# One w2 GEMM of a hybrid encoder layer: sums made in earlier jobs, and low parts moved between VectorE and adding transfers

## The chip, the cores and the metric

The kernel runs on one core of a Trainium2 chip. The metric is the device time of one execution in microseconds (us), as the median of several runs. The engines are named as the profile names them: PE (TensorE matmul), PEld (TensorE weight load), DVE (VectorE), ACT (ScalarE), POOL (GpSimd) and SP (SyncE, which here only issues transfers).

## What is computed

One layer of an encoder with 512 tokens of width 1024. It has two SwiGLU blocks, a recurrent branch and an attention branch. The change lies in the second SwiGLU block (FFN 2), which ends the layer:

```python
def swiglu(x, w1, w3, w2):
    return (jax.nn.silu(x @ w1) * (x @ w3)) @ w2

f = swiglu(rms_norm(h, ffn2_pre_g[l]), ffn2_w1[l], ffn2_w3[l], ffn2_w2[l])
h = h + 0.5 * rms_norm(f, ffn2_post_g[l])
```

Everything is float32; w1 and w3 are 1024 x 2816, w2 is 2816 x 1024. The hidden width is 22 blocks of 128, called f = 0 to 21.

## The kernel before

**Precision.** PE multiplies rounded operands. To keep float32 accuracy each operand is split into a high part (a rounded copy, made by ScalarE) and a low part (what the rounding left, made by VectorE as source minus high part: `split2`, L213 and L214). A product is three matmuls: high by high, low by high, high by low. A low part can also be made without VectorE: ScalarE writes the negated high part (or negated source), and a transfer issued by GpSimd adds the source onto it (`accum_op=ALU.add`, L610 and L613).

**Pair jobs.** w1 and w3 of FFN 2 run as 20 jobs of `Pairs` (f = 2 to 20 in steps of two, w1b and w3b in turn). Each job is a 2 x 2 block product in seven half-size products instead of eight, with sums of the weight blocks made by GpSimd (`S12`, `S34`) and split by ACT and DVE. `prep(m, i)` prepares a piece of the operands of job m and is called in the job before. Hooks (`late[n, i]`) run in job n behind its first, second or third product. The last job's hooks and its two `tail()` calls each ran `ahead`, which prepares one unit of the next stage; four units have slots of their own (`U_SLOTS`).

**w2 in halves.** `Halves` does the same seven-product scheme for w2 of FFN 2, with five groups of four hidden blocks (G = 5, `GS_B`), so 35 units, in the order m1, m5, m2, m6, m3, m7, m4 (`NAMES_B`). Units are numbered through: m1 is 0 to 4, m5 5 to 9, m2 10 to 14, m6 15 to 19, m3 20 to 24, m7 25 to 29, m4 30 to 34. The hidden blocks 20 and 21 (`TAIL_B`) are done by ordinary matmuls (`classical`). For each unit `prep` loads weight blocks (`raw_w2b`, 512 KB each), makes the high part `whi` (L607), the low part `wlo` (L615, or by transfer at L610 to L613) and the two parts of the x operand (`hx` for the first four units, then places in `uT`), and then `sums` makes, in place, the weight differences (T, L548: 128x1024) and the x sums (S, L551: 128x512) that later units need. For m1 that is T1 (b12 minus b11) and the sum s1. A unit is 12 matmuls of 512 columns (L640 to L642). `step(u)` prepares unit u + 5 (`LEAD`), runs the hooks of u and then the matmuls of u.

**What sets the order.** Nothing is reordered by a scheduler: each engine runs its instructions in the order in which the code issues them. Tiles in SBUF come from 42 equal slots (`NSLOT`), given out first in, first out: a new tile waits for the last use of the tile that had its slot before.

**The end.** `last_gemm` runs units 0 to 24, then for token tiles 0 and 1 the classical part, one or two preparations (units 29 and 30, then unit 31) and the norm of that tile (`post_norm`, L294 to L308, with ScalarE's squares at L296 and root at L259, and two output stores at L722). Then come m7 (units 25 to 29, in which units 32 and 33 are prepared and the last two tiles of h are loaded, L690), half of the classical part of token tiles 2 and 3, and `out("m7")` on VectorE (L652), which reads the PSUM banks that m4 then adds to. m4 runs twice, once for each of the token tiles 2 and 3 (six matmuls a unit); unit 34 is prepared when the first of the two begins. Each run of m4 is followed by the rest of that tile's classical part and its norm.

In this kernel m6's units 17 to 19 get their low parts by adding transfers (`M6_DMA`), m2's all five too, and m4's are made by VectorE.

Of the kernel before, what the change touches and what calls it, by code (L numbers as in the profile page):

```python
# [13 lines left out]
ALU = mybir.AluOpType  # L14
# [37 lines left out]
def hybrid_layer(ctx: ExitStack, tc: tile.TileContext, a: dict, out: bass.AP):  # L52
# [10 lines left out]
    def slot(shape, dt=F32, name="s"):  # L63
        uid[0] += 1
        return sb.tile(shape, dt, tag="slot", name=f"{name}_{uid[0]}")
# [9 lines left out]
    def f32(ap):  # L75
        return ap.bitcast(F32)
# [61 lines left out]
    raws, pairs = {}, {}  # L138
# [10 lines left out]
    def dma_to(n):  # L149
        while st["dma"] < min(n, len(order)):  # L150
            dma_one(st["dma"])
            st["dma"] += 1
# [11 lines left out]
    def split_to(n):  # L164
        while st["split"] < min(n, len(order)) and st["split"] not in paired:
            k = st["split"]
            dma_to(k + 1)
            r = raws.pop(k)
            if order[k] in BY_DMA:
                nm, i = order[k]  # L170
                pairs[k] = split_dma(r, a[nm][i * P : (i + 1) * P, :])
            else:
                hi = slot([P, D], F32R, name="whi")
                lo = slot([P, D], F32R, name="wlo")
                if order[k] in BY_POOL:
                    pool.tensor_copy(hi, r)
                else:
                    act.activation(hi, r, AF.Copy)
                dve.tensor_tensor(out=lo, in0=r, in1=f32(hi), op=ALU.subtract)
                pairs[k] = (hi, lo)  # L180
            st["split"] += 1
# [29 lines left out]
    def split2(hi, lo, src):  # L211

        act.activation(hi, src, AF.Copy)  # L213
        dve.tensor_tensor(out=lo, in0=src, in1=f32(hi), op=ALU.subtract)  # L214
# [276 lines left out]
    class Hidden:  # L491

        def __init__(self, seq):
            self.seq, self.f, self.t, self.done, self.eo = seq, {}, {}, 0, {}
# [21 lines left out]
    class Halves:  # L516
# [5 lines left out]
        def __init__(self, nm, hid, hooks, gs, names):  # L522
            self.nm, self.hid, self.hooks, self.gs, self.names = nm, hid, hooks, gs, names
            self.G = G = len(gs)
            self.loads = [(b, i) for bs in (("b11", "b12"), ("b22", "b21")) for i in range(G) for b in bs]
            if G > 4:
                self.loads[2 * G :] = [(b, i) for b in ("b22", "b21") for i in range(G)]
            self.cast_at = names.index("m3") * G - 5
            self.raw, self.ops, self.loaded, self.ready = {}, {}, 0, 0
            self.bank, self.c, self.accs, self.cast = {}, {}, {}, {}  # L530

        def src(self, b, i):
            src = a[self.nm]
# [19 lines left out]
        def t2(self, i):  # L553
            self.T("b22", "b22", "b12", i)
            del self.raw["b12", i]

        def sums(self, m, i):

            if m == "m1":
                self.T("b12", "b12", "b11", i)  # L560
                self.S((0, 1), (0, 1), (1, 1), i, ALU.add)
            elif m == "m5":
                if i < T2_EARLY:
                    self.t2(i)
                self.S((0, 0), (0, 1), (0, 0), i)
            elif m == "m2":
                if i >= T2_EARLY:
                    self.t2(i)
                self.T("b11", "b22", "b11", i)
                self.S((1, 0), (1, 0), (0, 0), i)  # L570
            elif m == "m6":
                self.S((0, 1), (1, 1), (0, 0), i)
                if self.G > 4:
                    self.T("b21", "b21", "b22", i)
                    del self.raw["b22", i]
            elif m == "m7":
                if self.G == 4:
                    self.T("b21", "b21", "b22", i)
                    del self.raw["b22", i]
                del self.raw["b11", i]  # L580
            elif m == "m4":
                del self.raw["b21", i]

        def prep(self, n):

            G = self.G
            while self.ready < min(n, 7 * G):
                u = self.ready
                self.ready += 1
                m, i = self.names[u // G], u % G  # L590
                self.load(min(4 * G, 2 * G + 1 + u))
                b, odd, half = self.OPERANDS[m]
                again = m == "m3" and G > 4
                hi = self.cast.pop(i) if m == "m3" and not again else slot([P, 2, 512], F32R, name="whi")
                lo = slot([P, 2, 512], F32R, name="wlo")
                if u < U_SLOTS:
                    xs = slot([P, 2, 2, 256], F32R, name="hx")
                else:
                    xs = uT[:, :, (u + 1) % 8, :].rearrange("p e (j c) -> p e j c", j=2)
                if again:  # L600
                    split2(hi, lo, self.cast.pop(i))
                elif m == "m3":
                    act.activation(lo, f32(hi), AF.Copy, scale=-1.0)
                    pool.dma_start(out=lo, in_=self.src(b, i), accum_op=ALU.add)
                else:
                    src = self.raw[b, i]
                    act.activation(hi, src, AF.Copy)  # L607
                    if m == "m2":
                        act.activation(lo, src, AF.Copy, scale=-1.0)
                        pool.dma_start(out=lo, in_=self.src(b, i), accum_op=ALU.add)  # L610
                    elif m == "m6" and i >= self.G - M6_DMA * (G > 4):
                        act.activation(lo, f32(hi), AF.Copy, scale=-1.0)
                        pool.dma_start(out=lo, in_=src, accum_op=ALU.add)  # L613
                    else:
                        dve.tensor_tensor(out=lo, in0=src, in1=f32(hi), op=ALU.subtract)  # L615
                split2(xs[:, 0, :, :], xs[:, 1, :, :], self.x(i, odd, half))
                self.ops[u] = hi, lo, xs
                if self.cast_at <= u < self.cast_at + G:
                    n = u - self.cast_at
                    if G > 4:  # L620
                        self.cast[n] = slot([P, 2, 512], name=f"raw_{self.nm}")
                        sp.dma_start(out=self.cast[n], in_=self.src("b22", n))
                    else:
                        self.cast[n] = slot([P, 2, 512], F32R, name="whi")
                        pool.dma_start(out=self.cast[n], in_=self.src("b22", n))
                self.sums(m, i)
# [53 lines left out]
    def blocks(nm, hid, pairs, late, h_src, gs, names, marks):  # L680

        hooks = {u: [] for u in range(7 * len(gs))}

        def tail_tile(n):
            hid.to(n + 1)
            split_to(st["get"] + n + 1)

        def h_back(t):
            h[t] = slot([P, D], name="h")
            sp.dma_start(out=h[t], in_=h_src(t))  # L690

        for at_, fn in zip(marks, (lambda n: dma_to(st["get"] + n + 1), tail_tile, h_back)):
            for n, u in enumerate(at_):
                hooks[u].append(lambda n=n, fn=fn: fn(n))
        half = Halves(nm, hid, hooks, gs, names)
        pairs.more = lambda n: half.load(LOAD_PAIRS[n])
        ahead = lambda: half.prep(half.ready + 1)
        end = len(pairs.jobs) - 1
        late[end, 1], late[end, 2 if pairs.R is None else 3] = [ahead], [ahead]
        pairs.run(ahead, late)  # L700
        return half

# [561 lines left out]
    def keep(u):  # L1264
        f, i = u // 2, u % 2
        if f not in kept:
            kept[f] = slot([P, 2, SEQ], name="kept")
        act.activation(kept[f][:, i, :], ps[u], AF.Copy)
# [34 lines left out]
    late = {(0, 1): [lambda: keep(2 * NC1 - 1)], (1, 1): [bias_in], (2, 3): [bias_parts], (3, 1): [bias_rows]}  # L1303
# [5 lines left out]

    h.clear()  # L1310
    half = blocks("w2a", hid, pairs_a, late, lambda t: a["x"][t * P : (t + 1) * P, :], GS_A, NAMES_A, MARKS_A)
    X1 = pairs_a = late = None
    for fn, at_ in zip((gate_kept, silu_kept, swiglu_kept), KEPT_AT):
# [5 lines left out]
    half = None  # L1319
# [185 lines left out]
    for t in range(NT):  # L1505
# [3 lines left out]
        for k in range(KT):  # L1509
            wh, wl = wv[k // 4]  # L1510
            s = slice((k % 4) * 256, (k % 4 + 1) * 256)
# [223 lines left out]
    late = {(0, 1): [lambda: X2.update(t4=to_uT(tn[3], 0, 1)), tn.clear]}  # L1735
    pairs_b.prep(1, 1)

    half = blocks("w2b", hid, pairs_b, late, lambda t: h_scr[t], GS_B, NAMES_B, MARKS_B)
    X2 = pairs_b = None
    last_gemm("w2b", hid, half, "ffn2_post_g", 0.5)  # L1740
# [29 lines left out]
LEAD = 5  # L1770
U_SLOTS = 4
LOAD_PAIRS = (0, 4, 6, 8)
GS_A = (1, 2, 3, 4)
NAMES_A = ("m1", "m5", "m2", "m6", "m7", "m3", "m4")
MARKS_A = (14, 16, 18, 20, 22, 24), (16, 18, 20, 22, 24, 26), (24, 25, 26, 27)
# [4 lines left out]
MARKS_B = (17, 18), (20, 22), (21, 22, 27, 29)  # L1780
GPOST_AT = 22
T2_EARLY = 3
M6_DMA = 3


RO = 6
# [59 lines left out]
```

## Time and profile before

| | |
|---|---|
| Median of 3 runs | 1113.86 us (1113.52 to 1114.41) |
| Profiled execution, its own time | 1112.68 us |
| Its span, first to last instruction | 1110.9 us |
| Granted TensorE clock, mean | 0.998 |
| First matmul of w2 of FFN 2 | 992.64 us from the span's start |
| Last matmul ends at | about 1104.2 us |

In the profile, a row of a timeline is: start, duration (both us), engine, line, operation, output and inputs, shape, and in brackets how long the engine had been idle before it and what ended that. A row of waits is: engine and line, what it waited for, total us, number of times, longest. A row of windows is: the window, its length, busy us (and instructions) of PE, PEld, DVE, ACT, POOL, then the granted clock, the share of the 16 DMA engines in use, and GB/s. A row of a transfer queue is: packets, MB, share of the 16 engines over the window. Recorded durations of DVE and ACT include an end that overlaps with the next instruction, so costs are taken from start to start.

### The profile page before, as it was taken

What the parts mean: (1) busy time and instruction counts of PE and PEld (TensorE: products, weight loads), DVE (VectorE), ACT (ScalarE), POOL (GpSimd) and SP (SyncE); (2) the same over time, 40 slices, a digit from 0 to 9 for tenths busy, and PEclk for the clock granted to TensorE, in tenths of its full rate; (3) what the DMA queues carried; (4) which work ended last, traced back from release to release, by engine and by line L of the source; (5) the groups of instructions that cost most, each with busy time, mean ns of one, the idle gap of its engine ahead of it and who ended that gap; (6) DMA issues with size and microseconds to landing.
All of it is one profiled execution on the core that took longest, in us unless ns stands there. A gap on an engine that the chain in (4) does not pass through costs nothing. (4 is left out here: it accounts for less than half of the span.)

```text
span 1110.9 us, 17989 instructions
## 1 busy us (share of the span) xinstructions
PE 1098.0 (99%) x6838; PEld 987.4 (89%) x6838; DVE 926.3 (83%) x1325; ACT 679.3 (61%) x1186; POOL 401.2 (36%) x332
## 2 busy tenths in 40 slices
PE   9999999999999999999999999999999999999996
PEld 7899999987788877899888888888999999997885
DVE  5888999999977978887778867767899898689995
ACT  7755556576747678666655664356455555567752
POOL 0143435602112423232556563010976665502000
PEclk9999999999999999999999999999999999999999
DMA  9325663477944542146122335442332323377712
GB/s 332 124 83 143 136 137 114 137 209 150 255 178 166 150 122 95 39 163 249 64 95 77 121 127 218 145 168 95 115 99 92 115 80 112 129 256 167 207 57 94
DMA packets 53061, 155.91 MB, mean 140 GB/s; under 512 B 5472, under 2 KB 7392, under 8 KB 52976
## 3 DMA queue, kind: packets, MB, share of 16 engines
q1 hardware_dynamic: 44128, 132.19, 34.5%
q0 software_dynamic: 8560, 22.07, 10.3%
q8 instruction: 53, 0.87, 0.3%
q10 hardware_dynamic: 288, 0.52, 0.1%
q14 instruction: 32, 0.26, 0.1%
HBM read 137.47 MB, written 13.62 MB: 136 GB/s over the span
## 5 line engine op out<-in xcount | busy, mean ns | idle before, releaser
L752 PE MATMUL c<-uT,wlo 128*128 128x256 f32 x516 | 146.0, 283 | 0.0
L753 PE MATMUL c<-uT,whi 128*128 128x256 f32 x516 | 146.0, 283 | 0.0
L751 PE MATMUL c<-uT,whi 128*128 128x256 f32 x516 | 146.0, 283 | 0.0
L752 PE MATMUL c<-Xh,wlo 128*128 128x256 f32 x504 | 142.8, 283 | 0.2 <-DVE wlo L214 0.2
L751 PE MATMUL c<-Xh,whi 128*128 128x256 f32 x504 | 142.7, 283 | 0.0
L224 PE MATMUL f<-uT,whi 128*128 128x512 f32 (+1 forms) x368 | 136.4, 371 | 0.0
L225 PE MATMUL f<-uT,wlo 128*128 128x512 f32 (+1 forms) x368 | 134.8, 366 | 0.0
L226 PE MATMUL f<-uT,whi 128*128 128x512 f32 (+1 forms) x368 | 134.8, 366 | 0.0
L753 PE MATMUL c<-Xl,whi 128*128 128x256 f32 x456 | 129.0, 283 | 0.0
L214 DVE TENSOR_TENSOR wlo<-S,whi 128x1024 fp32r<-128x1024 f32 x86 | 117.2, 1363 | 6.6 <-ACT whi L213 3.2
L213 ACT ACTIVATE whi<-S 128x1024 fp32r<-128x1024 f32 x86 | 88.5, 1054 | 33.2 <-DVE S L800 32.1
L752 PEld LDWEIGHTS c<-uT,wlo 128*128 128x128 f32 x516 | 99.0, 192 | 0.2
L751 PEld LDWEIGHTS c<-uT,whi 128*128 128x128 f32 x516 | 99.0, 192 | 0.2
L753 PEld LDWEIGHTS c<-uT,whi 128*128 128x128 f32 x516 | 99.0, 192 | 0.0
L752 PEld LDWEIGHTS c<-Xh,wlo 128*128 128x128 f32 x504 | 96.7, 192 | 0.5 <-DVE wlo L214 0.5
L751 PEld LDWEIGHTS c<-Xh,whi 128*128 128x128 f32 x504 | 96.7, 192 | 0.3 <-issue 0.3
L640 PE MATMUL hw<-whi,uT 128*128 128x512 f32 x220 | 85.9, 390 | 2.9 <-DVE hc L652 2.9
L753 PEld LDWEIGHTS c<-Xl,whi 128*128 128x128 f32 x456 | 87.5, 192 | 0.0
L641 PE MATMUL hw<-wlo,uT 128*128 128x512 f32 x220 | 86.5, 393 | 0.5 <-DMA wlo<-in_w2a_dram 0.2
L642 PE MATMUL hw<-whi,uT 128*128 128x512 f32 x220 | 86.3, 392 | 0.5
L224 PEld LDWEIGHTS f<-uT,whi 128*128 128x128 f32 x368 | 69.4, 189 | 12.5 <-issue 1.7
L226 PEld LDWEIGHTS f<-uT,whi 128*128 128x128 f32 x368 | 69.4, 189 | 11.4
(440 smaller groups left out, 3168.3 us busy)
## 6 DMA issues: line engine op xcount, KB each, us to landing
raw_w2b<-in_w2b_dram SPq DMA_DIRECT2D x27, 512.0 KB, 5.2
raw_w2a<-in_w2a_dram SPq DMA_DIRECT2D x22, 512.0 KB, 4.2
raw_w1b<-in_w1b_dram SPq DMA_DIRECT2D x22, 512.0 KB, 4.1
raw_w3b<-in_w3b_dram SPq DMA_DIRECT2D x22, 512.0 KB, 4.4
raw_w3a<-in_w3a_dram SPq DMA_DIRECT2D x21, 512.0 KB, 4.3
raw_w1a<-in_w1a_dram SPq DMA_DIRECT2D x20, 512.0 KB, 4.3
raw_wg<-in_wg_dram SPq DMA_DIRECT2D x16, 512.0 KB, 4.2
h<-in_x_dram SPq DMA_DIRECT2D x8, 512.0 KB, 7.3
```

Source lines behind the costliest of these rows:

```text
L213: act.activation(hi, src, AF.Copy)
L214: dve.tensor_tensor(out=lo, in0=src, in1=f32(hi), op=ALU.subtract)
L224: pe.matmul(ps[:, c0:c1], wh[:, s], h_, start=k == 0 and c0 == 0, stop=False, skip_group_check=True)
L225: pe.matmul(ps[:, c0:c1], wl[:, s], h_, start=False, stop=False, skip_group_check=True)
L226: pe.matmul(ps[:, c0:c1], wh[:, s], l_, start=False, stop=k == KT - 1, skip_group_check=True)
L640: pe.matmul(ps, xs[:, 0, j, c], hi[:, j, :], start=start and j == 0, stop=False, skip_group_check=True)
L641: pe.matmul(ps, xs[:, 0, j, c], lo[:, j, :], start=False, stop=False, skip_group_check=True)
L642: pe.matmul(ps, xs[:, 1, j, c], hi[:, j, :], start=False, stop=i == self.G - 1, skip_group_check=True)
L751: pe.matmul(ps, wh[:, s], xh, start=first, stop=False, skip_group_check=True)
L752: pe.matmul(ps, wl[:, s], xh, start=False, stop=False, skip_group_check=True)
L753: pe.matmul(ps, wh[:, s], xl, start=False, stop=k == 3, skip_group_check=True)
```

## The change

For w2 of FFN 2 alone (five groups; the four-group w2 of FFN 1 keeps its ways):

- The sums s1 of groups 0 to 3 and T1 of group 0 are made in the third pair job from the end, T1 of group 1 in the second from the end, T1 of group 2 in the last. `did` remembers them, so that `sums` leaves them out later; T1 of groups 3 and 4 and s1 of group 4 stay where they were.
- Unit 0 is prepared in the second job from the end, behind its second product, instead of in the last one. Units 1 to 3 follow in the last job.
- Six w2 loads are issued in the fourth job from the end (before: four at the end of the third from the end). The ones after that come later than before, relative to the units.
- m4's five low parts are made by a negation on ScalarE and an adding transfer, no longer by VectorE. m6's five are all made by VectorE; the three adding transfers there go.

```diff
+        def t1(self, i):
+            if ("t", i) not in self.did:
+                self.did.add(("t", i))
+                self.T("b12", "b12", "b11", i)
+
+        def s1(self, i):
+            if ("s", i) not in self.did:
+                self.did.add(("s", i))
+                self.S((0, 1), (0, 1), (1, 1), i, ALU.add)
+
         def sums(self, m, i):
             if m == "m1":
-                self.T("b12", "b12", "b11", i)
-                self.S((0, 1), (0, 1), (1, 1), i, ALU.add)
+                self.t1(i)
+                self.s1(i)
...
-        def prep(self, n):
+        def prep(self, n, load=True):
...
-                self.load(min(4 * G, 2 * G + 1 + u))
+                if load:
+                    self.load(min(4 * G, 2 * G + (u if u >= U_SLOTS else u == 3) if G > 4 else 2 * G + 1 + u))
...
-                    elif m == "m6" and i >= self.G - M6_DMA * (G > 4):
+                    elif m == "m4" and G > 4:
                         act.activation(lo, f32(hi), AF.Copy, scale=-1.0)
                         pool.dma_start(out=lo, in_=src, accum_op=ALU.add)
...
-        pairs.more = lambda n: half.load(LOAD_PAIRS[n])
-        ahead = lambda: half.prep(half.ready + 1)
+        pairs.more = lambda n: half.load((LOAD_PAIRS if len(gs) == 4 else LOAD_B)[n])
+        ahead = lambda: half.prep(min(half.ready + 1, U_SLOTS))
         end = len(pairs.jobs) - 1
         late[end, 1], late[end, 2 if pairs.R is None else 3] = [ahead], [ahead]
+        if pairs.R is None:
+            late[end - 3, 1] = [lambda: half.load(6)]
+            late[end - 2, 1] = [lambda i=i: half.s1(i) for i in range(len(gs) - 1)] + [lambda: half.t1(0)]
+            late[end - 1, 1] = [lambda: half.t1(1)]
+            late[end - 1, 2] = [lambda: half.prep(1, False)]
+            late[end, 1] = [lambda: half.t1(2)]
...
 LOAD_PAIRS = (0, 4, 6, 8)
+LOAD_B = (0, 6, 8, 10)
```

More of the change, by code (lines that the diff above doesn't have):

```diff
@@ L529, in __init__ @@
             self.raw, self.ops, self.loaded, self.ready = {}, {}, 0, 0
-            self.bank, self.c, self.accs, self.cast = {}, {}, {}, {}
+            self.bank, self.c, self.accs, self.cast, self.did = {}, {}, {}, {}, set()
         def src(self, b, i):
@@ L1782 @@
 T2_EARLY = 3
-M6_DMA = 3
 RO = 6
```

## The prediction

> **What bounds the kernel now.** The page first, then the waits of PE and of its weight loads in the last stage, then the timelines of that stage engine by engine, then its transfers.
>
> ```profile
> span 1110.9 us, 17989 instructions
> PE 1098.0 (99%) x6838; PEld 987.4 (89%) x6838; DVE 926.3 (83%) x1325; ACT 679.3 (61%) x1186; POOL 401.2 (36%) x332
> ...
> PE hw L640 <- DVE hc L652: 2.9, 1, 2.9
> ...
> PEld hw L641 <- DVE wlo L615: 1.3, 3, 0.5
> PEld hw L642 <- DVE uT L214: 1.2, 3, 0.4
> ...
> 1049.00:1069.00 20.00, 20.00 (x90) 16.57 (x89) 20.00 (x24) 14.37 (x20) 0.56 (x1) 1.00 0.23 80
> ```
>
> PE is the bound everywhere except in w2 of FFN 2 (from 992.6 us on). There VectorE (third busy time of the window's row) works 20.00 of 20 us, and PE waits for it: one stall of 2.9 us and six small weight-load waits, 2.5 us. More than some 5 us cannot be won.
>
> **The pair jobs, where work is added.**
>
> ```profile
> 962.42 1.68 POOL L804 TENSOR_TENSOR S<-raw_w3b 128x512 f32<-128x512 f32 x1 [1.49 <-DVE cc L874]
> ...
> 967.67 1.53 DVE L214 TENSOR_TENSOR wlo<-raw_w1b,whi 128x1024 fp32r<-128x1024 f32 x1 [4.73 <-ACT whi L213]
> ...
> 975.56 0.42 DVE L902 TENSOR_TENSOR hEO<-c,cc 128x256 f32<-128x256 f32 x1 [1.56 <-PE c L753]
> ...
> 977.28 2.00 ACT L213 ACTIVATE whi<-S 128x1024 fp32r<-128x1024 f32 x2
> ...
> 978.37 1.23 DVE L214 TENSOR_TENSOR wlo<-S,whi 128x1024 fp32r<-128x1024 f32 x1 [1.15 <-ACT whi L213]
> ...
> 981.74 0.42 DVE L874 TENSOR_TENSOR cc<-ct 128x256 f32<-128x256 f32 x1 [0.30 <-ACT ct L873]
> ...
> 984.12 1.23 DVE L615 TENSOR_TENSOR wlo<-raw_w2b,whi 128x1024 fp32r<-128x1024 f32 x1 [1.17 <-ACT whi L607]
> 985.27 0.68 DVE L214 TENSOR_TENSOR hx<-hEO,hx 128x512 fp32r<-128x512 f32 x1
> 985.87 1.22 DVE L548 TENSOR_TENSOR raw_w2b<-raw_w2b,raw_w2b 128x1024 f32<-128x1024 f32 x1
> 987.00 0.68 DVE L551 TENSOR_TENSOR hEO<-hEO,hEO 128x512 f32<-128x512 f32 x1
> ```
>
> Start to start, a 128x1024 operation takes 1.14 us and a 128x512 one 0.60. The third job from the end gets four x sums and one T1: 4 x 0.60 + 1.14 = 3.5 us, in a hole of 4.73. The one after gets a T1 in a hole of 1.56, then unit 0's two low parts (1.74); they push L902 back by about 1.7 us, and the 1.15 hole and the 0.30 one behind it take that up. So these cost PE nothing. Without the holes the cost would be their 6.4 us of queue.
>
> SP takes six w2 loads ahead of the last job's raw w3 weights. At under 0.5 us an issue (the row of the h loads below: 0.91 for two) that is under 3 us, for tiles that ScalarE reads over ten us later; nothing. The six loads hold six slots a job or two earlier: by my count of live tiles about 12 of the 42 are free there now, and about 5 would be. GpSimd's sums for the last job, which run a whole job ahead, then have to wait for slots (rival C).
>
> **How early VectorE gets.** In the last job it is held by what ScalarE has to do first.
>
> ```profile
> 987.34 0.39 ACT L850 ACTIVATE ct<-c 128x256 f32<-128x256 f32 x1
> ...
> 990.24 1.05 ACT L607 ACTIVATE whi<-raw_w2b 128x1024 fp32r<-128x1024 f32 x1
> ...
> 998.70 0.41 DVE L862 TENSOR_TENSOR cc<-c,ct 128x256 f32<-128x256 f32 x1
> ...
> 1000.42 1.22 DVE L615 TENSOR_TENSOR wlo<-raw_w2b,whi 128x1024 fp32r<-128x1024 f32 x1
> ...
> 1003.90 1.22 DVE L615 TENSOR_TENSOR wlo<-raw_w2b,whi 128x1024 fp32r<-128x1024 f32 x1
> ```
>
> Unit 2's high part still follows L850, which follows PE; unit 3's still starts at 990.24. So unit 3's low part starts at 991.35 at the earliest. Behind it: 1.14 + 0.60, T1 of unit 3 1.14, L862 to L902 1.72 (998.70 to 1000.42): unit 4 at 995.95, not 1000.42. Unit 4 keeps its T1 and sum (3.48, as from 1000.42 to 1003.90), so unit 5 starts at 999.4, not 1003.90. **Lead 4.5 us**, of 3 T1, 4 sums and one unit's splits, 7.6 us: the rest is lost in holes of the last job.
>
> Of the lead m6 takes three low parts that were transfers: 3 x 1.14 = 3.4. m4 gives one back before the first norm (unit 30): 1.1. At norm(0) VectorE is 4.5 - 3.4 + 1.1 = **2.2 us** earlier. The small PE waits mostly go, but PE isn't what is late:
>
> ```profile
> 1065.30 0.39 PE L244 MATMUL hw<-whi,hT 128*128 128x512 f32 x1
> ...
> 1069.78 0.68 DVE L294 TENSOR_TENSOR hc<-hw,hc 128x512 f32<-128x512 f32 x1
> ...
> 1078.07 0.68 DVE L294 TENSOR_TENSOR hc<-hw,hc 128x512 f32<-128x512 f32 x1
> ...
> 1086.79 1.28 DVE L652 TENSOR_TENSOR hc<-hw,hc 128x512 f32<-128x512 f32 x2
> ...
> 1087.62 0.47 PE L640 MATMUL hw<-whi,uT 128*128 128x512 f32 x1 [2.89 <-DVE hc L652]
> ```
>
> PE had the first token tile done at 1065.5, VectorE took it at 1069.78; from there to the stall the chain is VectorE's and ScalarE's.
>
> **From norm(0) to m4.** In m4 VectorE loses a 1.14 us low part per unit, and ScalarE gains a negation per unit.
>
> ```profile
> 1031.47 1.07 ACT L607 ACTIVATE whi<-raw_w2b 128x1024 fp32r<-128x1024 f32 x1 [0.40 <-DVE raw_w2b L548]
> 1032.57 1.06 ACT L612 ACTIVATE wlo<-whi 128x1024 fp32r<-128x1024 f32 x1
> 1033.54 0.61 ACT L213 ACTIVATE uT<-hEO 128x512 fp32r<-128x512 f32 x1
> ...
> 1074.32 1.04 ACT L607 ACTIVATE whi<-raw_w2b 128x1024 fp32r<-128x1024 f32 x1
> ...
> 1081.29 1.04 ACT L607 ACTIVATE whi<-raw_w2b 128x1024 fp32r<-128x1024 f32 x1
> ...
> 1083.71 0.61 ACT L213 ACTIVATE uT<-hEO 128x512 fp32r<-128x512 f32 x1
> ```
>
> m6 shows the form: negation 1.10 after the high part, x copy 0.97 after that, next unit 0.52 later, 2.59 us a unit instead of 1.47. Unit 31: high part at 1074.32 - 2.25 = 1072.07, x copy at 1074.14 to 1074.8, VectorE's x low part 0.60, norm(1) at 1075.4 instead of 1078.07: 2.67 earlier. Units 32 and 33 follow norm(1) on ScalarE: 1081.29 - 2.67 = 1078.62; unit 33's x copy at 1078.62 + 2.59 + 2.07 = 1083.28, done 1083.9. L652 is queued on VectorE behind that unit's x low part (1083.95 + 0.60): 1084.55 instead of 1086.79. m4 then starts at 1087.62 - 2.24 = **1085.38**. PE went idle at 1087.62 - 2.89 = 1084.73 and would, without some 1.9 us of small waits, at 1082.8: a stall of 2.5 us stays, and ScalarE is now its cause.
>
> **The adding transfers, the disputed term.** Unit 34's negation ends at 1078.62 + 2 x 2.59 + 1.10 + 1.06 = 1085.96; units 32 and 33 are 5.18 and 2.59 earlier.
>
> ```profile
> 1030.85 0.91 POOL L613 DMA_DIRECT2D wlo<-raw_w2b  x1 [4.71 <-ACT wlo L612]
> ...
> DMA to landing us min/median/max: 6.1/6.9/9.2
> ...
> 1010.99 1.26 POOL L610 DMA_DIRECT2D wlo<-in_w2b_dram  x1 [42.87 <-ACT uT L213]
> ...
> DMA  0000000000000000000058994966759366659599
> ...
> q0 software_dynamic: 432, 1.57, 57.4%
> ...
> 1083.85 0.91 SPq L690 DMA_DIRECT2D h<-h_scr  x2
> ...
> 1083.60:1088.20 4.60, 1.71 (x8) 1.11 (x8) 4.60 (x7) 2.19 (x4) 0.00 (x0) 1.00 0.98 337
> ...
> 1093.41 0.39 PE L641 MATMUL hw<-wlo,uT 128*128 128x512 f32 x1
> ```
>
> GpSimd issues 0.30 us after a negation (1032.57 is the second; the first ended at 1030.55, issue 1030.85). The digits are 0.1 us slices from 1010.9 us: the first bytes move 1.9 us after the issue. The q0 row covers 1032.7 to 1046.6: three transfers are 57.4% of 13.9 us, 2.66 us of all 16 engines each. Landing is 6.1 to 9.2 us after issue in m6, among reloads. In m4 the neighbours are norm(1)'s two output stores and the two loads of h, in the window's row 98% of all engines for 4.6 us; SP's order is kept, so with norm(1) they move to 1080.9 to 1085.5. Unit 32 issues at 1081.1, its bytes start at 1083.0, and 2.5 us of that traffic are still to come. Full engines then serve 2.5 + 3 x 2.66 = 10.5 us of work: 1093.5, and 0.3 to the landing (an estimate from the last m6 transfer): 1093.8. Unit 34's first L641 was 5.79 us behind m4's start (1093.41 - 1087.62) and so is due at 1091.17. It waits 2.7 us, to 1093.9 with 0.1 to restart, instead of 1093.41. Everything after that, 17 us of PE, norm(3) and stores, is unchanged.
>
> **Sum.** -2.24 + 2.7 = +0.5 us. The profiled execution took 1112.68 us, so 1113.2; the median stands 1.18 above it: **1114.4 us**. The transfer's bounds: 4.9 us from issue to landing (1.9 + 2.66 + 0.3, nothing beside it) gives unit 34 at 1091.3, -2.1 us in all; 9.2 gives 1095.6, +2.2. I take the middle because the stores and h loads do stand in its window.
>
> The Trainium skill, page "DMA: Bandwidth & Descriptors", section "Anatomy of one DMA — SWDGE (gpsimd) path", has about 2.0 us plus the bytes at 436 GB/s for a GpSimd transfer; an estimate from it for 0.52 MB is 3.2 us, by which no unit of m4 waits and the sum is rival A's. This trace, with 6.1 us at the least, does not agree.
>
> **Rivals.** A: the transfers are in time, m4 never waits. For it: units 30 and 31 issue long before, and a lone transfer misses by only 0.1 us. Against: 6.1 is the least seen. It gives -2.24: 1111.6 us. Chance 0.18.
> B: slower. Each transfer lands 9.2 us after its issue, as m6's third did behind its predecessor and four loads. Place: unit 34's first low product. Issued at 1086.26, unit 34's lands at 1095.5, and m4's first tile ends 2.2 us later than now: 1116.1 us. From 7.1 us on (1093.4) the change loses, from 9.2 on by over 0.2%. Chance 0.12.
> C: slower, in the pair jobs. With about 5 free slots GpSimd's sums for the last job wait until PE is through with this job's first operands, to the middle of the job, some 968 us, not 962.42, and take some 6 us; ScalarE reads them at 977.28. If they come over 3.5 us later still, PE stands in the last job and the lead is gone as well: some 2 to 4 us, 1117. Chance 0.12.
> The forecast itself, within 2.2 us of now, has 0.58.
>
> **How the numbers follow.** A change of 0.2% (2.2 us) is about what a measurement of this kernel can tell from none. Faster by over that: A, 0.18. Within it: 0.58. Slower: B and C, 0.24. The range takes in A and B, and leaves out C's upper half: 1111.3 to 1116.8.
>
> **What would show it.** Right: no DVE idle of 4.7 us in the third job from the end; unit 5's low part near 999.4; norm(0) near 1067.5; the stall at m4 still there, 2 to 3 us, and PE waiting for L613 transfers within m4's first token tile; three L613 transfers after 1080 us landing 7 us or more after issue. Wrong: a lead at norm(0) under 1 or over 3.5 us, no PE wait on wlo's transfers, or new PE waits before 992 us.

## The result, and the profile after

| | before | after |
|---|---|---|
| median of the runs compared | 1113.45 us (10 runs) | 1116.36 us (10 runs) |
| ratio | | 1.0026, 95% interval 1.0016 to 1.0036 |
| profiled execution, its span | 1112.68, 1110.9 us | 1116.02, 1114.0 us |
| first matmul of w2 of FFN 2 | 992.64 | 994.01 |
| m4's first matmul, counted from there | 94.98 | 92.65 |
| unit 34's first low product, counted from there | 100.77 | 102.35 |
| last matmul, counted from there | 111.20 | 112.92 |

The change makes the kernel 2.9 us slower, 0.26%: just over the 0.2% that the prediction took for a difference, with an interval that reaches below it, and inside the predicted range. Against the profile before, w2 of FFN 2 starts 1.4 us later and takes 1.7 us longer. In the table the middle of w2 went as predicted (m4 2.33 us earlier); the ends did not.

The page of the kernel after, and PE's waits in it from 945 us on (total, times, longest):

```profile
span 1114.0 us, 17982 instructions
...
PE 1097.9 (99%) x6838; PEld 987.7 (89%) x6838; DVE 929.5 (83%) x1323; ACT 682.1 (61%) x1188; POOL 406.8 (37%) x334
```

```profile
PE hw L652 <- DMA wlo<-raw_w2b: 3.2, 3, 1.2
PE hw L651 <- DVE hc L663: 2.1, 1, 2.1
PE c L769 <- DVE wlo L214: 1.6, 3, 0.7
```

Three kinds of waits. The second is the old stall ahead of m4, 0.8 us shorter (L663 is L652 of before). The first and the third are new. From start to start of the matmuls they are larger than in the row: the weight loads behind wait as well (4.5 and 2.2 us in their rows), and the next matmul of w2 starts 0.34 us behind the late one instead of 0.23. So counted, it is 4.0 us for the transfers and 2.4 us in the pair jobs. The matmuls at which this happens, in PE's timeline after, and the two ends of w2 before:

```profile
970.74 0.39 PE L769 MATMUL c<-uT,wlo 128*128 128x256 f32 x1 [0.42 <-DVE wlo L214]
...
972.97 0.39 PE L769 MATMUL c<-Xh,wlo 128*128 128x256 f32 x1 [0.54 <-DVE wlo L214]
...
982.52 0.39 PE L769 MATMUL c<-uT,wlo 128*128 128x256 f32 x1 [0.66 <-DVE wlo L214]
...
994.01 0.40 PE L651 MATMUL hw<-whi,hx 128*128 128x512 f32 x1
...
1086.66 0.47 PE L651 MATMUL hw<-whi,uT 128*128 128x512 f32 x1 [2.06 <-DVE hc L663]
...
1091.01 0.50 PE L652 MATMUL hw<-wlo,uT 128*128 128x512 f32 x1 [1.14 <-DMA wlo<-raw_w2b]
...
1093.82 0.51 PE L652 MATMUL hw<-wlo,uT 128*128 128x512 f32 x1 [1.16 <-DMA wlo<-raw_w2b]
...
1096.36 0.50 PE L652 MATMUL hw<-wlo,uT 128*128 128x512 f32 x1 [0.87 <-DMA wlo<-raw_w2b]
...
1106.93 0.39 PE L244 MATMUL hw<-whi,hT 128*128 128x512 f32 x1
```

```profile
992.64 0.40 PE L640 MATMUL hw<-whi,hx 128*128 128x512 f32 x1
...
1103.84 0.39 PE L244 MATMUL hw<-whi,hT 128*128 128x512 f32 x1
```

Behind the waits in the pair jobs stand GpSimd and VectorE. First GpSimd's S sums in the timeline after (they began at 953.46 and 962.42 before), then VectorE:

```profile
957.21 2.38 POOL L821 TENSOR_TENSOR S<-raw_w1b 128x512 f32<-128x512 f32 x1 [10.15 <-PE c L769]
...
967.40 2.19 POOL L821 TENSOR_TENSOR S<-raw_w3b 128x512 f32<-128x512 f32 x1 [2.45 <-PE c L770]
969.68 2.15 POOL L822 TENSOR_TENSOR S<-S,raw_w3b 128x512 f32<-128x512 f32 x1
971.91 2.16 POOL L816 TENSOR_TENSOR S<-raw_w3b,S 128x512 f32<-128x512 f32 x1
```

```profile
963.73 3.58 DVE L551 TENSOR_TENSOR hEO<-hEO,hEO 128x512 f32<-128x512 f32 x4
...
968.37 2.31 DVE L214 TENSOR_TENSOR wlo<-raw_w1b,whi 128x1024 fp32r<-128x1024 f32 x1
970.60 2.31 DVE L214 TENSOR_TENSOR wlo<-S,whi 128x1024 fp32r<-128x1024 f32 x1
...
978.05 1.21 DVE L548 TENSOR_TENSOR raw_w2b<-raw_w2b,raw_w2b 128x1024 f32<-128x1024 f32 x1
...
981.25 1.21 DVE L214 TENSOR_TENSOR wlo<-raw_w3b,whi 128x1024 fp32r<-128x1024 f32 x1
...
1000.78 1.22 DVE L626 TENSOR_TENSOR wlo<-raw_w2b,whi 128x1024 fp32r<-128x1024 f32 x1
...
1068.92 0.70 DVE L294 TENSOR_TENSOR hc<-hw,hc 128x512 f32<-128x512 f32 x1
...
1076.75 0.68 DVE L294 TENSOR_TENSOR hc<-hw,hc 128x512 f32<-128x512 f32 x1
...
1085.83 1.28 DVE L663 TENSOR_TENSOR hc<-hw,hc 128x512 f32<-128x512 f32 x2
```

GpSimd waits for PE, 10.15 us ahead of the first sum: for slots that PE still reads, as the sixth and ninth experiments bear out. Its sums for the last job then run to 976.3 us, beside the low parts of the job before it, and the first two of those take 2.31 us instead of 1.21: PE waits for them at 970.74 and 972.97. The third wait, at 982.52, is for the last job's first low part (981.25). GpSimd is through by then; on VectorE that low part stands behind a T1 (978.05) and unit 0's two low parts, and VectorE comes to them late. The row at 1000.78 is unit 5's low part, 6.77 us behind the first w2 matmul; before it was 11.26 behind.

And the transfers of 1082 to 1100 us after (queues: packets, MB, share of 16 engines; issues: KB each, median us to landing), with the landings of all five of m4 (min/median/max):

```profile
q0 software_dynamic: 432, 1.57, 44.0%
q1 hardware_dynamic: 576, 1.57, 30.8%
...
wlo<-raw_w2b POOLq DMA_DIRECT2D x3, 512.0 KB, 8.8
h<-h_scr SPq DMA_DIRECT2D x2, 512.0 KB, 7.0
...
DMA to landing us min/median/max: 4.4/8.6/8.8
```

q0 is GpSimd's queue, q1 SP's. By the packet records q0 moves no byte until 1086.13 us, 3.7 us after unit 32's issue at 1082.40. Until then only q1 does, 0.94 MB in 94% of all engines over 1082.00 to 1086.12, with one gap: from 1084.00 to 1084.55 no packet starts on any queue.

### The profile page after: what moved, and what is told of

Same layout as the page of the kernel before. It is cut to its first block, busy times and chain, and to the rows that moved or that the text cites. A ratio compares the mean times of both kernels' runs of the same rounds, so it can differ in the third digit from the quotient of the medians.

```text
span 1114.0 us, 17982 instructions
## 1 busy us (share of the span) xinstructions
PE 1097.9 (99%) x6838; PEld 987.7 (89%) x6838; DVE 929.5 (83%) x1323; ACT 682.1 (61%) x1188; POOL 406.8 (37%) x334
## 5 line engine op out<-in xcount | busy, mean ns | idle before, releaser
L214 DVE TENSOR_TENSOR wlo<-S,whi 128x1024 fp32r<-128x1024 f32 x86 | 118.4, 1377 | 6.0 <-POOL OL L1658 3.1
L652 PE MATMUL hw<-wlo,uT 128*128 128x512 f32 x220 | 86.4, 393 | 3.4 <-DMA wlo<-raw_w2b 3.2
```

The costliest lines, as they stand in the source:

```text
L652: pe.matmul(ps, xs[:, 0, j, c], lo[:, j, :], start=False, stop=False, skip_group_check=True)
```

## The experiments

The theory: the early loads make GpSimd's sums late and cost PE 2.4 us in the pair jobs; m4's transfers are held back by SP's stores and h loads and cost 4.0 us; the lead of VectorE is real and is spent on the exchange of low parts. The rivals: VectorE's added operations cost PE by themselves; the transfers are slow by themselves. The first, second, fourth and fifth kernels start from the full change, the others from an earlier experiment; ratios are to the kernel before.

**1. Two early loads instead of six.**

```diff
-            late[end - 3, 1] = [lambda: half.load(6)]
+            late[end - 3, 1] = [lambda: half.load(2)]
-LOAD_B = (0, 6, 8, 10)
+LOAD_B = (0, 4, 6, 10)
```

> The change with two early w2 loads instead of six, the other four made in the last pair job as far as its slots allow. Slot theory (the six loads hold slots that GpSimd's S sums for the last pair job wait for; late sums put a 128x1024 low part of VectorE beside GpSimd's work at 2.3 us instead of 1.2, and PE waits for wlo of L214 three times, 2.4 us in all): the sums of the last job start near 962 to 963 us instead of 967.4, PE's waits for L214's low parts before w2 of FFN 2 fall from 2.4 us to under 0.5, w2 starts 2 us earlier, and the time is 2 us below the full change, some 0.9 us above the kernel before. Rival (VectorE's added sums and T1 themselves delay the low parts): GpSimd's sums come early, but PE still waits 1.5 to 2.4 us for L214, and the time is that of the full change.

1116.15 us, ratio 1.0022 (1.0013 to 1.0030): no gain that can be told. GpSimd's timeline:

```profile
955.03 1.29 POOL L821 TENSOR_TENSOR S<-raw_w1b 128x512 f32<-128x512 f32 x1 [7.41 <-PE c L770]
...
965.17 1.72 POOL L821 TENSOR_TENSOR S<-raw_w3b 128x512 f32<-128x512 f32 x1 [2.13 <-PE c L770]
```

The sums are still released by PE, only 2.2 us earlier, and two low parts behind the four x sums and the T1 still stand beside them: PE waits 1.6 us (2.1 from start to start). The expectation missed: two loads still hold slots, and both theories stay.

**2. m4's low parts by VectorE too; no adding transfer in m4 or m6.**

```diff
-                    elif m == "m4" and G > 4:
+                    elif m == "m0":
```

> The change without any adding transfer in w2 of FFN 2: m4's low parts by VectorE too. Theory (m4's transfers start only when norm(1)'s stores and the two h loads have gone, and cost PE 4.0 us of waits): PE has no wait on a transfer for wlo; norm(0) comes some 1.1 us later than with the change (one low part of unit 30 more on VectorE), m4 starts 0.5 us earlier to 0.5 later since ScalarE loses its negations, and the time is about 2.7 us below the full change: 0.2 us above the kernel before. Rival (PE would wait in m4 anyway, for low parts that VectorE now makes one behind the other): waits on DVE wlo in m4 of 2 us or more take the place of the transfers' and the time stays within 1 us of the full change.

1115.24 us, ratio 1.0011 (1.0000 to 1.0023). PE's one wait in w2, and the windows around it (busy us of PE, PEld, DVE, ACT and POOL, PE's granted clock, share of DMA, GB/s):

```profile
PE hw L651 <- DVE hc L663: 3.3, 1, 3.3
```

```profile
1088.00:1092.00 4.00, 0.73 (x3) 0.64 (x3) 4.00 (x7) 1.47 (x3) 0.00 (x0) 0.77 0.95 322
1092.00:1096.00 4.00, 4.00 (x11) 3.14 (x10) 2.93 (x5) 0.72 (x2) 0.00 (x0) 0.50 0.01 2
```

The waits for transfers are gone and no low part is waited for. But VectorE has lost 1.1 us ahead of norm(0) and the stall grew by as much, to 3.3; behind it PE ran at half clock for 5.7 us in this execution, the longest of the twelve (1119.67 us). The gain is 1.7 us where 2.7 were expected. The six executions at a mean clock of 0.998 took 1112.7 to 1115.7 us, the five at 0.995 or 0.996 1115.6 to 1119.7, so a part of what is missing is probably lost clock.

**3. The pair-job part alone: two early loads, low parts as in the kernel before.**

```diff
-                    elif m == "m4" and G > 4:
+                    elif m == "m6" and i >= self.G - 3 * (G > 4):
```
with the edits of the first experiment.

> The x sums and T1 in the pair jobs alone, with two early loads instead of six, and the low parts as in the kernel before: m6's last three by adding transfers, all of m4's by VectorE. Theory (the lead of 4.5 us that VectorE gets in the pair jobs is real, and m6's low parts and m4's transfers spend it): norm(0) and norm(1) come 4 to 4.5 us earlier than in the kernel before, the stall of 2.9 us ahead of m4 goes to under 0.5, PE's small waits of 2.5 us fall to 0.5, and the time is 4 to 4.5 us below the kernel before: ratio 0.996. Rival (the lead is used up by other waits on the way, of ScalarE or of m6's transfers, which now have less time): norm(0) less than 2.5 us earlier and a time within 2 us of the kernel before.

1110.56 us, ratio 0.9970 (0.9959 to 0.9982), faster than both kernels. w2 takes 106.71 us from its first matmul to its last, 4.5 less than before. PE's timeline at m4:

```profile
1085.88 0.47 PE L651 MATMUL hw<-whi,uT 128*128 128x512 f32 x1 [0.16 <-DVE hc L663]
```

The lead is real, and where it isn't spent it comes out as time. The pair jobs still wait 2.1 us here.

**4. The change, with the two last h loads four and five units earlier.**

```diff
-MARKS_B = (17, 18), (20, 22), (21, 22, 27, 29)
+MARKS_B = (17, 18), (20, 22), (21, 22, 23, 24)
```

> The change with the two last loads of h made four to five units earlier, so that they don't stand in the window of m4's adding transfers; norm(1)'s stores stay. Theory (m4's transfers are held back by SP's traffic, stores and h loads, to 1086.1 us): issue to landing of the three last transfers falls from 8.6 us to 5 to 6.5, PE's waits for them from 4.0 us to 0 to 1.5, and the time is 2.5 to 4 us below the full change, 0.4 above to 1.1 below the kernel before. Rival (the transfers take that long by themselves, 2.7 us of all engines each one behind the other): landing stays at 8 us or more, the waits at 3 us or more, and the time is that of the full change.

1113.29 us, ratio 0.9992 (0.9983 to 1.0001): 3.8 us less than the full change by the ratios. Its transfers of 1082 to 1100 us:

```profile
q0 software_dynamic: 432, 1.57, 44.3%
q1 hardware_dynamic: 378, 0.71, 10.2%
...
wlo<-raw_w2b POOLq DMA_DIRECT2D x3, 512.0 KB, 4.5
```

Same 44% of the engines for the same bytes, 4.5 us to landing instead of 8.8, and PE waits for none of them. It was the neighbours on SP's queue, not the transfers' own work.

**5. The six loads, but nothing added in the third job from the end.**

```diff
-            late[end - 2, 1] = [lambda i=i: half.s1(i) for i in range(len(gs) - 1)] + [lambda: half.t1(0)]
+            late[end - 2, 1] = []
```

> The change with its six early w2 loads, but without the four x sums and the T1 in the third job from the end (they are made in w2 of FFN 2, as before). Port theory (GpSimd's S sums and VectorE's two-input operations hold each other up: 2.31 us instead of 1.21 for a 128x1024 low part, 2.16 instead of 1.30 for a sum; the loads make the sums late and put them beside the low parts, the added sums do so too): GpSimd's sums stay late, at 967 us, low parts still take 2.3 us beside them, and PE still waits 0.5 to 1.5 us for L214's low parts before w2. Rival (VectorE's added operations alone): no PE wait there. By both, VectorE loses 3.5 us of its lead, the stall ahead of m4 grows from 2.2 to about 5 us, and the time is 1 to 3 us above the full change.

1117.79 us, ratio 1.0036 (1.0022 to 1.0049). PE's wait in the pair jobs:

```profile
PE c L769 <- DVE wlo L214: 2.2, 1, 2.2
```

With nothing added in that job PE waits all the same: one wait of 2.2 us, in the last job. GpSimd's sums are as late as in the change (957.36 and 967.56 us), which makes VectorE late, and the T1 and sum that fall back into unit 0's preparation come on top. The stall did not grow (2.1 us): unit 5's low part is only 0.7 us later in w2. That half of the expectation missed: the five operations of that job buy little lead; the last two jobs' holes take most of them when they come later. The time is 1.1 us above the full change by the ratios, with intervals that overlap.

**6. Third experiment without any early load; T1 of the first three groups in the last two jobs.**

```diff
-            late[end - 3, 1] = [lambda: half.load(2)]
-            late[end - 2, 1] = [lambda i=i: half.s1(i) for i in range(len(gs) - 1)] + [lambda: half.t1(0)]
-            late[end - 1, 1] = [lambda: half.t1(1)]
+            late[end - 2, 1] = [lambda i=i: half.s1(i) for i in range(len(gs) - 1)]
+            late[end - 1, 1] = [lambda: half.t1(0)]
             late[end - 1, 2] = [lambda: half.prep(1, False)]
-            late[end, 1] = [lambda: half.t1(2)]
+            late[end, 1] = [lambda: half.t1(1)]
+            late[end, 2] = [ahead, lambda: half.t1(2)]
```

> As the third experiment (low parts as in the kernel before), but with no early w2 loads: the four x sums stay in the third job from the end, the T1 of the first three groups go to the last two jobs. Slot theory (the loads alone make GpSimd's sums late): GpSimd's sums for the last job start at 962 to 963 us again, no PE wait for L214's low parts, time 2 us below the third experiment. Port theory: GpSimd starts at 962 to 963 us, but its sums and VectorE's take turns to about 969 us, the low part behind them starts 1 us later than in the kernel before, and PE waits 0.5 to 1.2 us (2.1 in the third experiment); time 1 us below the third experiment.

1108.29 us, ratio 0.9952 (0.9938 to 0.9966), 2.0 us below the third by the ratios. GpSimd, then VectorE:

```profile
961.90 1.67 POOL L821 TENSOR_TENSOR S<-raw_w3b 128x512 f32<-128x512 f32 x1 [1.50 <-DVE cc L891]
```

```profile
962.34 6.91 DVE L551 TENSOR_TENSOR hEO<-hEO,hEO 128x512 f32<-128x512 f32 x4
969.17 1.21 DVE L214 TENSOR_TENSOR wlo<-raw_w1b,whi 128x1024 fp32r<-128x1024 f32 x1
```

GpSimd is on time again, released by VectorE and not by PE. The four sums now share the whole hole with it and take 6.91 us, not 2.4; yet PE waits nowhere in the pair jobs, though the low part behind them starts 2.0 us later than before (1.5 in the rows, and this execution is 0.5 us ahead). The slot theory holds for GpSimd's start; the wait of 0.5 to 1.2 us expected from turns taken beside GpSimd did not come. For PE's wait the test is not a clean one, since T1 of group 0 left that job together with the loads. Here the low part is ready at 970.38 and PE reads it at 970.62; with the T1's 1.14 us in front of it PE would have waited some 0.9 us even with GpSimd on time (an estimate from these rows). No run has that T1 there without early loads.

**7. As the sixth, x sums spread over four jobs.**

```diff
-            late[end - 2, 1] = [lambda i=i: half.s1(i) for i in range(len(gs) - 1)]
+            for i in range(len(gs) - 1):
+                late[end - 8 + 2 * i, 1] = [lambda i=i: half.s1(i)]
```

> As the one before it, but with the four x sums spread, one in each of the last four jobs of the same kind (w3's). Port theory: 0.6 us of VectorE work beside 5.4 us of GpSimd's sums moves the next low part by 0.6 us at the most, as far as such low parts are moved in the kernel before already (1.53 and 1.61 us instead of 1.21), and PE waits nowhere for L214: time 2 us below the third experiment, about 5.5 us below the kernel before (ratio 0.995). Rival (each added operation is paid on PE wherever it stands, 0.6 us each): waits of 0.3 to 0.6 us in each of four jobs, time as the third experiment's or above.

1107.89 us, ratio 0.9949 (0.9935 to 0.9962): not to be told from the sixth. PE's only wait from 945 us on:

```profile
PE hw L651 <- DVE hc L663: 0.5, 1, 0.5
```

The sums stand in the four w3 jobs ahead of the last. Clumped or spread, they are free when GpSimd is on time. This is the best version, 5.7 us below the kernel before by the ratio, and half a us is left of PE's waits in this stage.

**8. As the fourth, and m4 splits x ahead of w2's high part.**

```diff
                     src = self.raw[b, i]
+                    if m == "m4" and G > 4:
+                        split2(xs[:, 0, :, :], xs[:, 1, :, :], self.x(i, odd, half))
                     act.activation(hi, src, AF.Copy)
...
-                split2(xs[:, 0, :, :], xs[:, 1, :, :], self.x(i, odd, half))
+                if m != "m4" or G == 4:
+                    split2(xs[:, 0, :, :], xs[:, 1, :, :], self.x(i, odd, half))
```

> As the fourth experiment (the change with the two h loads made early), and in m4 the split of x is made ahead of w2's high part and negation on ScalarE. ScalarE theory (the stall ahead of m4 is set by ScalarE's order, 2.6 us a unit, since L663 stands on VectorE behind the x low part of unit 33): L663 starts 2 to 2.5 us earlier, the stall of 2.1 us ahead of m4 goes to under 0.3; but unit 34's transfer is issued no earlier and lands about 1092.7 us, so PE waits there 1 to 1.8 us, and the time falls by 0.3 to 1 us only. Rival (norm(1)'s own chain on VectorE sets the stall): L663 within 0.7 us of where it was, stall still above 1.4 us, same time.

1112.32 us, ratio 0.9990 (0.9981 to 0.9999). VectorE's timeline (L666 is L663 here), then PE's waits in w2:

```profile
1083.58 1.28 DVE L666 TENSOR_TENSOR hc<-hw,hc 128x512 f32<-128x512 f32 x2
```

```profile
PE hw L655 <- DMA wlo<-raw_w2b: 1.0, 1, 1.0
PE hw L655 <- DMA wlo<-in_w2b_dram: 0.9, 1, 0.9
```

L663 comes 2.9 us earlier than in the fourth (1086.45) and the stall ahead of m4 is gone: ScalarE's order caused it. At once unit 34 waits for its transfer (1.0 us), and another 0.9 comes in m2, for one of its transfers from w2 in DRAM. The ratio is the fourth's within its interval. The stall had been cover for the transfers.

**9. The seventh with the six early loads put back.**

```diff
+            late[end - 3, 1] = [lambda: half.load(6)]
-LOAD_B = (0, 4, 6, 10)
+LOAD_B = (0, 6, 8, 10)
```

> The kernel with the x sums spread (the seventh experiment), and only the six early w2 loads put back. Slot theory (the loads take the slots that GpSimd's S sums wait for): the sums of the last two jobs start at 957 and 967 us, released by PE, not at 954 and 962 to 963; low parts beside them take 2.2 to 2.3 us; PE waits 1.5 to 2.4 us for L214's low parts, and the time is 1.5 to 2.5 us above the kernel with the sums spread. Rival (the loads cost only together with the four sums and the T1 in the third job from the end): waits under 0.5 us, same time.

1109.36 us, ratio 0.9963 (0.9949 to 0.9976). GpSimd, then PE's wait in the pair jobs:

```profile
957.64 2.38 POOL L823 TENSOR_TENSOR S<-raw_w1b 128x512 f32<-128x512 f32 x1 [8.11 <-PE c L771]
...
967.84 1.64 POOL L823 TENSOR_TENSOR S<-raw_w3b 128x512 f32<-128x512 f32 x1 [2.45 <-PE c L772]
```

```profile
PE c L771 <- DVE wlo L214: 0.5, 1, 0.5
```

The loads alone make the sums late, as the theory has it; but alone that costs PE 0.5 us in the pair jobs (0.7 from start to start), not 1.5 to 2.4. The times differ by 1.5 us with intervals that overlap. This wait is at the start of the last job, where the change's third one (0.9 us from start to start) is, behind a T1 and unit 0's preparation, as there. The two waits in the job before, 1.5 us in the change, came only with the four sums and the T1 of group 0 in front, never with the six loads alone (the fifth experiment and this one).

**10. The seventh with the exchange of low parts put back.**

```diff
-                    elif m == "m6" and i >= self.G - 3 * (G > 4):
+                    elif m == "m4" and G > 4:
```

> The kernel with the x sums spread, and only the exchange of low parts put back: m6's all by VectorE, m4's by adding transfers, the h loads where they were. Theory (the exchange by itself costs: the lead goes to m6's low parts, ScalarE's negations set the stall ahead of m4, and SP's stores and h loads hold the transfers back): no PE wait in the pair jobs; from the first w2 matmul on as in the full change, that is 6 us longer than with the sums spread: the stall 2.2 us, transfer waits 3.5 to 4.2 us; time 5.5 to 6.5 us above the kernel with the sums spread, 2 us below the full change. Rival (with VectorE earlier there is slack, and the exchange costs under 3 us): time within 3 us of the kernel with the sums spread.

1114.37 us, ratio 1.0005 (0.9995 to 1.0015): 6.2 us above the seventh by the ratios, 2.3 below the full change. PE's waits from 945 us on, and the windows of m4:

```profile
PE hw L651 <- DVE hc L663: 2.1, 1, 2.1
PE hw L652 <- DMA wlo<-raw_w2b: 1.9, 2, 1.0
```

```profile
1084.00:1088.00 4.00, 2.74 (x7) 2.17 (x8) 3.30 (x6) 2.61 (x4) 1.26 (x2) 0.71 1.00 252
1088.00:1092.00 4.00, 3.43 (x13) 2.46 (x11) 0.55 (x2) 0.42 (x2) 0.00 (x0) 0.86 1.06 235
```

No wait in the pair jobs; w2 takes 112.88 us, as in the full change (112.92), where the seventh takes 106.71. The stall is as expected; of the transfers' waits one is hidden, because PE ran at half clock until 1089 us here. The exchange costs some 6 us in both pairs of kernels that differ in it alone (this one and the seventh: 6.2; the first and the third: 5.8 by the ratios), and the difference between this kernel and the full change is the pair jobs.

## Why the prediction was right or wrong

**The bound, and VectorE's lead: right.** Unit 5's low part is 4.5 us earlier within w2 (6.77 us after the first matmul, before 11.26): the 4.5 predicted. The third and tenth experiments show what it is worth by itself and that the exchange spends it: w2 of 106.71 us against 112.88. The third's w2 is 4.5 us shorter than before, within the bound of some 5.

**From norm(0) to m4: right.** m4 starts 2.33 us earlier within w2; predicted 2.24. The stall stayed, 2.1 us in PE's row (2.5 predicted), and the eighth experiment shows that ScalarE's order of high part, negation and x copy is its cause.

**The pair jobs, "these cost PE nothing", loads "nothing": the step that failed.** PE waited 2.4 us there. (w2 starts only 1.37 us later, because this execution was 1.0 us ahead at 950 us, in code that the change doesn't touch.) Rival C had named the mechanism: few free slots, GpSimd's sums at "some 968 us"; they came at 967.40. What it had wrong was the way from there to PE. It let the sums cost something only if ScalarE got them 3.5 us later still. What they cost is VectorE: its low parts beside them take 2.31 us instead of 1.21. The hole of 4.73 us in which the four sums were to hide was the time of GpSimd's sums, 962.42 to 968.1 in the profile before: I read it as free, on VectorE alone. It is still free enough for the sums when GpSimd is on time (sixth and seventh experiments); it wasn't with the T1 there as well and GpSimd moved behind it by six loads, or by two. One of the prediction's own signs of being wrong, new PE waits before 992 us, thus came. A slip in the same step changes nothing: a T1 and 1.74 us in a hole of 1.56 push L902 back by 1.3 us, not 1.7.

The Trainium skill, page "SBUF — State Buffer", section "Who interferes with whom", says that a VectorE instruction with two inputs in SBUF and a GpSimd instruction that reads SBUF exclude each other for the whole of an instruction. The traces agree: in the rows of after the two start one of theirs every 2.2 us in turn, a GpSimd sum takes 2.16 us there and a VectorE low part 2.31, where alone they take 1.30 and 1.21.

**The adding transfers, 2.7 us: mis-sized, 4.0 measured.** Each takes 2.64 us of all engines (44.0% of 18 us for three), as the 2.66 predicted, and unit 32's issue came where the step put it within w2 (1082.40 - 994.01 = 88.4 us behind the first matmul; the step had 1081.1 - 992.64 = 88.5). The stores and h loads ahead of them were to take 4.5 us of all engines and took 5.5 (30.8% of 18). The step let unit 32's bytes start 1.9 us behind its issue and share the engines with what was left of that traffic; they started 3.7 us behind it, when 0.94 of the traffic's 1.57 MB had moved. Unit 34's first low product therefore came 1.58 us later within w2, not 0.5. The bound of 4.9 us for a transfer with nothing beside it was good: 4.4 to 5.0 in the fourth experiment, with the stores alone near them and no wait in m4, which is rival A's case. The estimate of 3.2 us from the Trainium skill, page "DMA: Bandwidth & Descriptors", is below all of them.

**The sum.** Predicted: 0 in the pair jobs, -2.24, +2.7. By the trace: +1.37 at w2's start, -2.33, +3.9 to unit 34, +0.1 behind it: +3.1 us, and +2.9 in the medians. The chances had 0.24 on a loss of over 0.2% and this is one, by a hair; it came by a piece of rival C and a larger transfer term together. That the time lies in the range, 0.4 us under its upper end, is owed to the range's width: neither of these two terms was right.

**Partly settled:** why six loads that alone cost 0.7 us and sums that alone cost nothing make 2.4 together. By the timelines the lateness adds up on VectorE. The last low part of the second job from the end (L214, raw_w1b) starts some 3.4 us late in the fifth experiment, by GpSimd's late sums alone, and 5.1 us late in the change (975.93 and 977.45 against 973.33, these executions being 0.85 and 1.0 us ahead); unit 0 and a T1 behind it then use up what PE had to spare. What the T1 of group 0 alone would cost was not run.

## What to carry to other kernels

A hole in VectorE's timeline beside GpSimd's sums is smaller than it looks (four sums took 6.91 us in it instead of 2.4): lay the two timelines beside each other before putting work into it, and look at what moves either of them. An early load is paid in slots, and the price shows on the engine that wants the next slot, not on the queue that loads. Before work is handed to transfers, list what other queues move in that window; here moving two loads by four and five units was worth 3.8 us.

## What the runs showed of the hardware

**A stall can cost PE more than its length.** In the second and tenth experiments (and in the first), after stalls of 3.3 and 2.1 us ahead of m4, the matmuls that followed started every 0.43 us instead of 0.23, for 5.7, 3.6 and 3.4 us, at granted clocks down to 0.50 and 0.71 in the windows above; after stalls of 2.0 and 2.1 us the full change and the fourth and fifth experiments kept full clock. The Trainium skill, page "TensorE: Matmul & The Clock Gate", section "Part 1: The HAM clock gate", has PE's clock halved after an idle window of about 3.4 us that runs freely; the halving agrees, the length doesn't: 2.1 us of waiting was enough here in two executions. In the first comparison the mean granted clock of the kernel before was 0.996 or 0.997 in 26 of 30 runs, of 1113.4 to 1115.9 us, and 0.998 in four of 1111.5 to 1112.1; in the later comparisons the two groups overlap. It probably pays for its stall of 2.9 us in this way in most runs, which its profiled execution, at 0.998, doesn't show, and which would be why the seventh experiment wins 5.7 us by the ratio and 4.5 us by w2's traces.

**A transfer of GpSimd's queue can start late beside SP's.** With stores and h loads on the engines, unit 32's transfer moved its first byte 3.7 us after its issue, against 1.9 us for a transfer with free engines in the profile before; from 1086.13 us on the two queues shared. That is no rule: m6's first transfer in the profile before, issued at 1030.85 us while SP's loads kept all engines busy, moved its first byte after 1.9 us at the latest. Nor were the engines full all the time here, by the gap at 1084 us. The fourth experiment shows that the h loads cost the time; why the start came so late is open.
